# Attention scores in three fp32r passes, conv tails copied by GpSimd, an earlier first feed-forward, two loads moved and a new table of held steps in a hybrid decoder layer on one core

## The chip, the cores and the metric

One Trainium2 chip, one of its cores. The time of a run is device microseconds from the start to the end of the program on that core. Three runs of the kernel before took 3500.38, 3508.79 and 3495.04 us (median 3500.38). A change of 0.5% is 17.5 us.

## The reference, cut to what matters

One decoder layer is computed for a prompt of 2048 tokens and, beside it, for eight single sample tokens with caches. D = 1024, eight heads of 128: four of a gated DeltaNet group (a short convolution over time, then a delta-rule state) and four of a sparse attention group (two key-value heads; a lightning indexer chooses 256 keys for each query).

```python
qkv, z, beta_in, a_in, aq, ak, av, iq, ik, iw = jnp.split(h @ w_in, cuts, axis=-1)
conv = sum(w_conv[i] * xcat[:, i:i + t] for i in range(CONV_W))      # CONV_W = 4
...
s = jnp.einsum('bqgrd,bqkgd->bqgrk', qg, ks).astype(jnp.float32) * d ** -0.5
s = jnp.where(valid[:, :, None, None, :], s, -jnp.inf)
p = jax.nn.softmax(s, axis=-1).astype(vs.dtype)
...
x = x + ga1 * mixed
gate, up = jnp.split(h2 @ w_ffn_in, 2, axis=-1)
x = x + ga2 * ((jax.nn.silu(gate) * up) @ w_ffn_out)
```

The attention scores `s` are the product that the change computes in another way. For the prompt the kernel computes them for all keys up to the query and adds a bias of 0 or -1e30 that the indexer's selection gives.

## The kernel before, in words

**Tiles and stages.** The prompt is worked in four groups g of 512 tokens (`GT`). The stages are: modulation vectors; for each group the projections of the normed input by `w_in` (`project`), with the convolution, the delta rule in chunks of 128 tokens and the indexer's keys beside them; then for each group the output projection and the feed-forward (`ffn`), with the attention of 16 query blocks of 128 (`index`, `attend`) and the sample tokens' work beside them. Blocks 0 to 3 are attended early, during the projections (`first_attn`); blocks 4 to 15 in the second phase.

**Products.** Large products are done as three fp32r passes (`mm3`): both operands are split in a part that fp32r holds and the rest, and high by high, high by low and low by high are added in PSUM. In the profile these are L201, L202 and L203. A product whose operands are plain fp32 (the scores, L1799) is one matmul in the program, and two records of TensorE in the trace. A weight tile is loaded (`wr`, L183), cast by ScalarE to its high part (L184), and the rest taken by VectorE (L185); three pairs are kept (`WI`). The last feed-forward group uses a longer ring for pairs: `wi` and, in turns, tiles of the tags `kT` and `V`, which attention no longer needs, three of each (`KR`).

**Order.** `weave` runs several streams: `feeds` (projections, then feed-forwards), `chain` (delta rule, early attention), `toks` (rotary, transposes and stores of projected rows, from a queue), later `samples`, `indices` and `attends`. Each is a generator that yields a planned cost and a wait; the planner picks the next step that is able. The matmuls are then bound to stand on TensorE in exactly the order in which the steps came (`o`), so that a matmul whose data is late holds everything behind it. On the other engines and on SP, which issues nearly all DMAs, a scheduler orders the instructions. A table `DELAY` names, for a stream and a step's number, how many planned microseconds that stream is held after that step, so that other streams' steps go first.

**What the steps below touch.** `conv` reads a projected block from PSUM (`pd`, tag `d`, four banks): three ScalarE copies, of the last three columns of the group before (L975), of the block (L976) and of its own last three columns, from PSUM, to `hist` (L977). `tok` transposes the rotated queries and keys and stores them to `qT_d` and `kT_d` (L1030, L1048). `attend` loads them back (L1788, L1795), computes a score (L1799), and VectorE adds the bias and takes the maximum (L1800). `modulation` loads at the start, in SP's order, half of two parts of `w_ada` (`hh`, then `hl`) and the four row tiles of group 0 (`xt`, L336). `projects` ends with a wait for the queue of `toks` to be empty, and `ffn(0)` comes after it.

Of the kernel before, what the change touches and what calls it, by code (L numbers as in the profile page):

```python
# [20 lines left out]
try:  # L21
# [4 lines left out]
F32 = mybir.dt.float32  # L26
# [8 lines left out]
T = 2048  # L35
# [21 lines left out]
KR = 3  # L57
RB = 2
WR, WI = 2, 3
S2, S4, LATE = 8, 1044, 8000  # L60
# [6 lines left out]
    "attends": {18: 5.36, 27: 5.03, 43: 0.99},  # L67
    "chain": {6: 0.3, 7: 0.13, 16: 1.19, 44: 0.99, 45: 2.33, 48: 1.66, 57: 0.53, 62: 1.14, 110: 0.7, 112: 0.9, 124: 2.17, 162: 0.55, 163:
        0.36, 190: 0.44, 200: 0.23, 213: 0.85, 215: 3.15, 246: 0.89, 248: 2.32, 257: 3.29, 297: 0.55, 298: 0.36, 313: 0.29, 326: 1.4, 342:
        0.5, 354: 0.25, 442: 0.55, 443: 0.56, 455: 0.51, 460: 2.84, 461: 0.68, 483: 0.18, 492: 0.45, 508: 0.31, 515: 1.71, 517: 0.92, 536:  # L70
        0.21},
    "feeds": {1: 2.29, 14: 1.6, 27: 0.45, 101: 1.94, 182: 1.01, 451: 0.69, 457: 1.65, 588: 0.89, 714: 5.33, 902: 1.81, 903: 0.53, 1084:
        12.87, 1085: 0.65, 1197: 0.88, 1259: 1.05, 1290: 5.26, 1354: 0.8, 1355: 1.08, 1386: 1.28, 1389: 1.47, 1450: 2.45, 1451: 1.77, 1482:
        6.57},
    "indices": {2: 7.17},
    "samples": {2: 1.37, 4: 1.91, 8: 3.28, 13: 3.31, 17: 2.24, 29: 0.3, 40: 1.93},
    "toks": {1: 1.91, 5: 6.16, 79: 3.96, 106: 0.46, 134: 1.8, 136: 4.86, 184: 0.56, 193: 3.29, 229: 3.52, 231: 1.66, 239: 2.29, 241: 1.22,
        246: 1.66},
# [51 lines left out]
class K:  # L130
# [106 lines left out]
    def build(self):  # L237
        tc, nc = self.tc, self.nc
        with ExitStack() as es:
# [3 lines left out]
            self.qT_d = self.dr.tile([NB, 128, H * 128], F32, name="qT_d")  # L243
            self.iqT_d = self.dr.tile([NB, 128, 8 * 128], F32, name="iqT_d")
            self.kT_d = self.dr.tile([2, 128, T], F32, name="kT_d")
# [71 lines left out]
    def modulation(self):  # L317
# [17 lines left out]
        for t in range(4):  # L335
            nc.sync.dma_start(self.x0[:, t, :], A["x_prompt"][0, t * 128:(t + 1) * 128, :])  # L336
        self.load_ada(hl, 1, 0, 0, KB)
# [341 lines left out]
    def projects(self):  # L679
        nxt = None  # L680
        for g in range(self.ng):
# [59 lines left out]
    def project(self, g, rows):  # L741
# [10 lines left out]

        if samp:
# [4 lines left out]
        hidden(0)  # L758
        yield TP, 0.5
        hidden(1)  # L760
        yield TP, 2
# [4 lines left out]
        for c in range(3):  # L766
# [3 lines left out]
            for k in range(KB):  # L770
# [200 lines left out]
    def conv(self, g, m, pd):  # L971
# [3 lines left out]
        nc.scalar.copy(raw[:, 0:3], self.hist[:, m, :])  # L975
        nc.scalar.copy(raw[:, 3:515], pd)  # L976
        nc.scalar.copy(self.hist[:, m, :], pd[:, 509:512])  # L977
# [31 lines left out]
    def tok(self, what, blk, a, rows):  # L1009
# [8 lines left out]
        if what == "aq":  # L1018
# [9 lines left out]
            q = self.m("qo")[:, :512]  # L1028
            nc.scalar.copy(q, pt)
            nc.sync.dma_start(self.qT_d[blk], q)  # L1030
            yield TP, 0
        elif what == "kv":
# [13 lines left out]
            q = self.m("qo")[:, :512]  # L1046
            nc.scalar.copy(q[:, :256], pt[:, :256])
            nc.sync.dma_start(self.kT_d[:, :, tk].rearrange("h p n -> p h n"), q[:, :256].rearrange("p (h n) -> p h n", h=2))  # L1048
# [34 lines left out]


# [217 lines left out]
    def out_T(self, n, o):  # L1302
# [9 lines left out]
        raw = self.m("ol")[:, :512]  # L1312
# [22 lines left out]
    def sample_gdn(self):  # L1335
# [19 lines left out]
        for c in range(3):  # L1355
# [3 lines left out]
            yield 0, 4  # L1359
# [352 lines left out]
    def buffers(self):  # L1712
# [3 lines left out]
        return dict(pool=p, kT=one("kT", 512, KR), V=one("V", 512, KR), ikT=self.ikT, qT=one("qT", 512), iqT=one("iqT", 1024), sc=one("sc", T + 18, 2),  # L1716
# [3 lines left out]
    def first_attn(self, i0):  # L1720
# [8 lines left out]
        B = dict(pool=p, kT=one("E"), V=one("AT"), ikT=ikT, qT=one("qe"), iqT=one("sq", 1024), sc=lambda: p.tile([128, 528], F32, name="ct", tag="ct", bufs=4),  # L1729
# [53 lines left out]
    def attend(self, i, B, bias):  # L1783
# [3 lines left out]
        qT = B["qT"]().rearrange("p (h n) -> p h n", h=H)  # L1787
# [438 lines left out]
```

## Time and profile before

| | |
|---|---|
| the profiled execution | 3502.24 us |
| its span, first to last instruction | 3499.8 us |
| mean granted TensorE clock | 0.973 |
| TensorE busy | 3300.3 us, 94% of the span |
| TensorE weight loads, VectorE, ScalarE, GpSimd busy | 75%, 59%, 42%, 18% |
| moved by DMA | 549.7 MB, mean 157 GB/s |

Busy time of TensorE is the union of its records. A record lasts until the result has drained, while the next has begun, so a group's mean of 400 ns for a 512-column fp32r pass is no price: the price is the distance of starts. The granted clock of a stretch is 1.00 or, in parts, one half; a stretch's mean says how much of it was at half rate. Waits are those of the engine that is named first; "SPq" is the queue from which DMAs are issued. Line numbers are those of the kernel before, unless it is said that they are of the changed one.

### The profile page before, as it was taken

Reading aid. Unit: us, or ns where it says so; the run is one execution under the profiler, and the core shown is the slowest. Engines: PE = TensorE matmul, PEld = TensorE weight load, DVE = VectorE, ACT = ScalarE, POOL = GpSimd, SP = SyncE. Lnnn points to the kernel's source line nnn. Section 1 sums busy time; section 2 is a strip of 40 time slices with the busy share of each in tenths; the row PEclk is TensorE's granted clock in tenths of the full one; section 3 lists DMA queues with packets and bytes.
Section 4 is the critical chain, followed back from the end, with each engine's and each line's share of the span. In section 5 each row is a group of like instructions: output and inputs, shape, how many; then the busy total and the mean of one; then the engine's idle time right before and its main releaser. Section 6 shows DMA issues by size and latency. Waiting matters only on the chain.

```text
span 3499.8 us, 61968 instructions
## 1 busy us (share of the span) xinstructions
PE 3300.3 (94%) x22852; PEld 2623.9 (75%) x22852; DVE 2076.9 (59%) x4488; ACT 1470.0 (42%) x2875; POOL 640.8 (18%) x633
## 2 busy tenths in 40 slices
PE   7899998999998899999998999999899999999997
PEld 5677777777766777777776777787777777789996
DVE  4656545645744656666676656567766763554434
ACT  4333322423433333455546555454645553342323
POOL 1001000100000113221220122212112221324335
PEclk8999999999998999999999999999999999999999
DMA  8865764675786254455464345335423233622221
GB/s 287 272 204 167 247 210 147 220 244 171 230 282 208 92 163 120 138 168 166 125 212 139 102 144 171 106 105 197 143 88 113 91 111 94 202 82 88 88 91 56
DMA packets 421019, 549.70 MB, mean 157 GB/s; under 512 B 50020, under 2 KB 287817, under 8 KB 420698
## 3 DMA queue, kind: packets, MB, share of 16 engines
q1 hardware_dynamic: 420690, 545.62, 48.9%
q8 instruction: 182, 2.98, 0.4%
q14 instruction: 131, 1.07, 0.1%
q10 hardware_dynamic: 16, 0.03, 0.0%
HBM read 441.78 MB, written 122.70 MB: 161 GB/s over the span
## 4 chain that ended last, share of the span: by engine, by line
PE 71%; DMA 9%; DVE 9%; issue 5%; ACT 4%; SPq 1%; POOL 1%; ACTq 0%; DVEq 0%; POOLq 0%
PE d L201 16%; PE d L203 15%; PE d L202 15%; PE s L1754 3%; PE g L1816 3%; PE s L1799 3%; DMA wr<-in_w_ffn_in_dram 2%; DMA wi<-kept 1%; DVE wi L185 1%; PE g L1828 1%; PE s L202 1%; PE s L201 1%; PE s L203 1%; ACT bias L1623 1%; ACT wi L184 1%
## 5 line engine op out<-in xcount | busy, mean ns | idle before, releaser
L201 PE MATMUL d<-hh,wi 128*128 128x512 f32 (+1 forms) x1616 | 669.8, 414 | 20.2 <-DVE th L2153 7.6
L185 DVE TENSOR_TENSOR wi<-wr,wi 128x512 fp32r<-128x512 f32 x525 | 391.9, 747 | 396.9 <-ACT wi L184 392.4
L202 PE MATMUL d<-hl,wi 128*128 128x512 f32 (+1 forms) x1616 | 620.7, 384 | 4.7 <-DVE hl L506 4.4
L203 PE MATMUL d<-hh,wi 128*128 128x512 f32 (+1 forms) x1616 | 620.8, 384 | 0.0
L184 ACT CAST wi<-wr 128x512 fp32r<-128x512 f32 x525 | 324.6, 619 | 680.9 <-PE d L203 427.1
L201 PEld LDWEIGHTS d<-hh,wi 128*128 128x128 f32 x1616 | 308.3, 191 | 94.0 <-issue 11.7
L202 PEld LDWEIGHTS d<-hl,wi 128*128 128x128 f32 x1616 | 308.8, 191 | 68.4 <-issue 10.1
L203 PEld LDWEIGHTS d<-hh,wi 128*128 128x128 f32 x1616 | 307.6, 190 | 62.1 <-DVE wi L185 0.8
L201 PE MATMUL d<-wi,hh 128*128 128x512 f32 x736 | 317.6, 432 | 17.5 <-DMA wi<-kept 7.7
L202 PE MATMUL d<-wi,hh 128*128 128x512 f32 x736 | 291.9, 397 | 1.0 <-DVE wi L185 1.0
L203 PE MATMUL d<-wi,hl 128*128 128x512 f32 x736 | 292.4, 397 | 0.0
L201 PE MATMUL d<-wi,ah 128*128 128x512 f32 x616 | 267.9, 435 | 10.7 <-ACT ah L2161 5.0
L203 PE MATMUL d<-wi,al 128*128 128x512 f32 x616 | 246.9, 401 | 2.4 <-POOL al L2162 2.4
L202 PE MATMUL d<-wi,ah 128*128 128x512 f32 x616 | 245.9, 399 | 0.0
L2162 POOL TENSOR_TENSOR al<-ca,ah 128x512 fp32r<-128x512 f32 (+1 forms) x88 | 107.6, 1228 | 732.1 <-ACT ah L2161 698.3
L1763 DVE SCALAR_TENSOR_TENSOR sc<-rl,iw,sc 128x512 f32<-128x512 f32 (+3 forms) x224 | 173.3, 774 | 73.4 <-ACT rl L1756 67.8
L1891 POOL TENSOR_TENSOR xt<-xt,tm 128x512 f32<-128x512 f32 x96 | 136.9, 1441 | 426.3 <-DVE tm L1890 341.0
L1756 ACT ACTIVATE rl<-s 128x512 f32<-128x512 f32 (+3 forms) x288 | 151.5, 543 | 135.2 <-PE s L1754 126.6
L201 PEld LDWEIGHTS d<-wi,hh 128*128 128x128 f32 x736 | 140.3, 191 | 61.1 <-DMA wi<-kept 11.3
L1623 ACT ACTIVATE bias<-sc,sv 128x640 bf16<-128x640 f32 (+11 forms) x120 | 169.9, 1416 | 26.9 <-DVE sv L1625 15.1
L1754 PE MATMUL s<-ik,iqT 128*128 128x512 f32 (+3 forms) x576 | 171.2, 391 | 3.9 <-DVE st L1800 2.3
L203 PEld LDWEIGHTS d<-wi,hl 128*128 128x128 f32 x736 | 140.4, 191 | 32.2 <-issue 0.3
(587 smaller groups left out, 6323.8 us busy)
## 6 DMA issues: line engine op xcount, KB each, us to landing
wi<-kept SPq DMA_DIRECT2D x168, 512.0 KB
wr<-in_w_ffn_in_dram SPq DMA_DIRECT2D x584, 128.0 KB
wr<-in_w_ffn_out_dram SPq DMA_DIRECT2D x148, 256.0 KB
kept<-wi SPq DMA_DIRECT2D x56, 512.0 KB
row<-in_w_ada_dram SPq DMA_DIRECT2D x32, 512.0 KB
wr<-in_w_in_dram SPq DMA_DIRECT2D x56, 256.0 KB
xt<-in_x_prompt_dram SPq DMA_DIRECT2D x7, 2048.0 KB
kT<-kT_d SPq DMA_DIRECT2D x54, 256.0 KB
```

What stands on the lines that cost most here:

```text
L184: nc.scalar.copy(hi, wr)
L185: nc.vector.tensor_tensor(lo, wr, hi.bitcast(F32), op=OP.subtract)
L201: self.o(nc.tensor.matmul(out, wh, xh, start=start, stop=False, **kw))
L202: self.o(nc.tensor.matmul(out, wh, xl, start=False, stop=False, **kw))
L203: self.o(nc.tensor.matmul(out, wl, xh, start=False, stop=stop, **kw))
L1623: nc.scalar.activation(c, s, AF.Sign, bias=t, accum_out=cnt)
L1754: self.o(nc.tensor.matmul(ps[:, :w], iq[:, h, :].bitcast(F32R), B["ikT"][c * 2 + a][:, :w].bitcast(F32R), start=a == 0, stop=a == 1))
L1756: nc.scalar.activation(r[:, :w], ps[:, :w], AF.Relu)
L1763: nc.vector.scalar_tensor_tensor(s, r[:, :w], iw, s, op0=OP.mult, op1=OP.add)
L1799: self.o(nc.tensor.matmul(ps[:, :w], qT[:, h, :], kT[:, :w], start=True, stop=True))
L1891: (nc.vector if soon else nc.gpsimd).tensor_tensor(xt, xt, tm, op=OP.add)
L2162: nc.gpsimd.tensor_tensor(al[b][:, cs], a, ah[b][:, cs].bitcast(F32), op=OP.subtract)
```

## The change

- **Scores.** `parts` splits the transposed queries and keys in two fp32r parts (ScalarE casts, VectorE subtracts, both from PSUM); both are stored and loaded, so `qT_d`, `kT_d` and their loads double. The score is `mm3` in place of one fp32 matmul. Key tiles hold two parts each, and there are two of them (`RK`) in place of three; the last feed-forward's ring has two double tiles there in place of three pairs. To make room, the samples' tile ring goes from eight to six (`S2`).
- **Conv tails.** The two three-column copies go to GpSimd, and the second reads the SBUF copy instead of PSUM. `out_T` writes its raw tile over its input.
- **First feed-forward.** `projects` no longer waits for the queue; for the last group the modulation steps start earlier (`"mark"` in the conv loop); the gates' column has a tile of its own.
- **Moves.** At the start the second `w_ada` load goes ahead of the fourth row tile; the sample rows are prepared after the first two `hidden` tiles. The samples' first step is held 9 planned us instead of 4.
- **Table.** `DELAY` keeps its entries and gains or lengthens 55, by 69.7 planned us in sum. Steps of `feeds` are counted anew where steps were added, so old entries stand at up to some steps' distance from their old places.

```diff
-S2, S4, LATE = 8, 1044, 8000
+RK = 2
+S2, S4, LATE = 6, 1044, 8000
 DELAY = {
-    "attends": {18: 5.36, 27: 5.03, 43: 0.99},
+    "attends": {18: 5.36, 27: 5.03, 41: 2.04, 43: 0.99, 109: 1.17, 119: 0.16, 120: 0.98, 137: 0.48, 280: 0.28},
...
-    "samples": {2: 1.37, 4: 1.91, 8: 3.28, 13: 3.31, 17: 2.24, 29: 0.3, 40: 1.93},
+    "samples": {2: 1.37, 4: 1.91, 8: 7.09, 13: 3.31, 17: 2.24, 21: 5.15, 29: 0.3, 40: 1.93, 134: 0.53, 154: 1.89},
...
         for t in range(4):
+            if t == 3:
+                self.load_ada(hl, 1, 0, 0, KB)
             nc.sync.dma_start(self.x0[:, t, :], A["x_prompt"][0, t * 128:(t + 1) * 128, :])
-        self.load_ada(hl, 1, 0, 0, KB)
...
-                col = self.m("gate")
+                col = self.p1.tile([128, 8], F32, name="gcol", tag="gcol", bufs=1)
...
-        yield lambda: not self.queue
         self.ready.add("end")
...
                 if c == 0:
                     hidden(k + 2)
                     yield TP * (k + 2 < KB), 0
+                elif k % 2 and g == self.ng - 1:
+                    yield "mark"
...
-        nc.scalar.copy(raw[:, 0:3], self.hist[:, m, :])
+        nc.gpsimd.tensor_copy(raw[:, 0:3], self.hist[:, m, :])
         nc.scalar.copy(raw[:, 3:515], pd)
-        nc.scalar.copy(self.hist[:, m, :], pd[:, 509:512])
+        nc.gpsimd.tensor_copy(self.hist[:, m, :], raw[:, 512:515])
...
-            nc.scalar.copy(q, pt)
-            nc.sync.dma_start(self.qT_d[blk], q)
+            for e, q in enumerate(self.parts(pt, 512)):
+                nc.sync.dma_start(self.qT_d[blk, :, e], q)
...
+    def parts(self, pt, w):
+
+        nc = self.nc
+        hi, lo = [self.m("qo", F32R)[:, :w] for _ in range(2)]
+        nc.scalar.copy(hi, pt[:, :w])
+        nc.vector.tensor_tensor(lo, pt[:, :w], hi.bitcast(F32), op=OP.subtract)
+        return hi.bitcast(F32), lo.bitcast(F32)
...
-            yield 0, 4
+            yield 0, 4 if c else 9
...
-                nc.sync.dma_start(kT[:, :w], self.kT_d[kv, :, c * 512:c * 512 + w])
+                for e in range(2):
+                    nc.sync.dma_start(kT[e][:, :w].bitcast(F32), self.kT_d[kv, :, e, c * 512:c * 512 + w])
...
-                    self.o(nc.tensor.matmul(ps[:, :w], qT[:, h, :], kT[:, :w], start=True, stop=True))
+                    self.mm3(ps[:, :w], *[x[:, h * 128:(h + 1) * 128] for x in qT], *[x[:, :w] for x in kT], True, True)
...
-                    yield F4 * w / 512, 0, dict(dve=0.2 + 0.6 * w / 512, use="s", need="s")
+                    yield 3 * MM * w / 512, 0, dict(dve=0.2 + 0.6 * w / 512, use="s", need="s")
...
-            return [q.tile([128, 512], F32R, name=tag, tag=tag, bufs=KR) for tag in ("kT", "V")]
+            w = q.tile([128, 2, 512], F32R, name="kT", tag="kT", bufs=RK)
+            return w[:, 0], w[:, 1]
```

How the change moves instructions is shown at three places; names are those of tiles, and line numbers those of the kernel in question. Lines 201 to 203 of before are lines 203 to 205 of the changed kernel, and other lines move by 2 to 16.

**TensorE, end of the last projections.** Before, after the last projection's matmuls (`s<-cf,iqs`: transposes of `toks`; `g<-ct`, `g<-Dm,E`: the delta rule's chunks):

```order
L450 MATMUL s<-cf,m_11923 128x32 x4
L1183 MATMUL g<-cf,ct 128x128 x8
L1234 MATMUL g<-ct 128x256 x4
L1078 MATMUL s<-cf,iqs 128x128 x4
L1234 MATMUL g<-ct 128x256 x4
L1078 MATMUL s<-cf,iqs 128x128 x4
L1112 MATMUL g<-Dm,E 32x32 x32
```

The changed kernel, same place:

```order
L1245 MATMUL g<-ct 128x256 x4
L203 MATMUL d<-wi,hh 128x512
L204 MATMUL d<-wi,hh 128x512
L205 MATMUL d<-wi,hl 128x512
L1245 MATMUL g<-ct 128x256 x4
L1081 MATMUL s<-cf,iqs 128x128 x4
```

The first feed-forward's passes now stand between the steps of `chain` and `toks`, which stood alone.

**TensorE, a score of block 4 to 7.** Before, and then in the changed kernel:

```order
L1754 MATMUL s<-ik_14241,iqT 128x256
L1754 MATMUL s<-ik_14242,iqT 128x256
L1799 MATMUL s<-kT,qT 128x512
L201 MATMUL d<-wi,ah 128x512
L202 MATMUL d<-wi,ah 128x512
```

```order
L205 MATMUL d<-hh,wi 128x512
L203 MATMUL s<-kT,qT 128x512
L204 MATMUL s<-kT,qT 128x512
L205 MATMUL s<-kT,qT 128x512
L1419 MATMUL g<-s_17057,s_17966 128x1 x4
```

One score is three instructions; what stands beside it differs, since all streams' places have moved.

**SP, the first loads.** Before, and then in the changed kernel:

```order
L333 DMA gzc<-in_g_gdn_norm_dram 1x128
L336 DMA xt<-in_x_prompt_dram 128x1024 x4
L359 DMA hl<-in_w_ada_dram 128x4x512 x2
L339 DMA row<-in_x_sample_dram 8x1024
L183 DMA wr<-in_w_in_dram 128x512 x2
```

```order
L335 DMA gzc<-in_g_gdn_norm_dram 1x128
L340 DMA xt<-in_x_prompt_dram 128x1024 x3
L362 DMA hl<-in_w_ada_dram 128x4x512 x2
L340 DMA xt<-in_x_prompt_dram 128x1024
L342 DMA row<-in_x_sample_dram 8x1024
```

The second `w_ada` load stands one row tile earlier.

More of the change, by code (lines that the diff above doesn't have):

```diff
@@ L66 @@
 DELAY = {
[L67 to L78 removed]
+    "attends": {18: 5.36, 27: 5.03, 41: 2.04, 43: 0.99, 109: 1.17, 119: 0.16, 120: 0.98, 137: 0.48, 280: 0.28},
+    "chain": {5: 0.79, 6: 0.3, 7: 0.13, 16: 1.19, 19: 0.75, 44: 0.99, 45: 2.33, 48: 1.66, 56: 0.3, 57: 0.53, 61: 0.23, 62: 1.14, 85: 0.36,
[3 rows of a table added]
+    "feeds": {1: 2.29, 14: 1.6, 27: 0.45, 101: 1.94, 102: 1.07, 142: 2.08, 182: 1.01, 451: 0.69, 457: 1.65, 588: 0.89, 636: 1.12, 711: 0.69,
[3 rows of a table added]
+    "indices": {2: 7.17, 14: 5.43, 16: 1.62, 78: 0.28, 223: 2.29, 249: 0.54},
+    "samples": {2: 1.37, 4: 1.91, 8: 7.09, 13: 3.31, 17: 2.24, 21: 5.15, 29: 0.3, 40: 1.93, 134: 0.53, 154: 1.89},
+    "toks": {1: 1.91, 5: 6.16, 43: 0.47, 67: 0.56, 77: 0.18, 79: 3.96, 106: 1.56, 134: 1.8, 136: 4.86, 139: 0.82, 184: 0.56, 187: 0.56, 193:
+        3.29, 196: 0.45, 229: 3.52, 231: 1.66, 239: 2.29, 241: 1.22, 246: 1.66},
 }
@@ L751, in hidden @@
                 self.hidden_T(k, xt, hh, hl, self.A1, B1, "s", 2)
+        hidden(0)
+        yield TP, 0.5
+        hidden(1)
+        yield TP, 0.5
         if samp:
@@ L757, in project @@
             held = []
[L758 to L761, printed above, removed]
+        yield 0, 1.5
         def wtile(k, c0):
@@ L1045, in tok @@
                 return
-            q = self.m("qo")[:, :512]
-            nc.scalar.copy(q[:, :256], pt[:, :256])
-            nc.sync.dma_start(self.kT_d[:, :, tk].rearrange("h p n -> p h n"), q[:, :256].rearrange("p (h n) -> p h n", h=2))
+            for e, q in enumerate(self.parts(pt, 256)):
+                nc.sync.dma_start(self.kT_d[:, :, e, tk].rearrange("h p n -> p h n"), q.rearrange("p (h n) -> p h n", h=2))
             nc.sync.dma_start(self.V_d[tk], a[:, 256:512])
@@ L1311, in out_T @@
             self.o(nc.tensor.transpose(pt[:, hs(h)], o[:, hs(h)], self.id))
-        raw = self.m("ol")[:, :512]
+        raw = o
         lo = raw.bitcast(F32R)
@@ L1715, in buffers @@
         one = lambda tag, w, bufs=1, dt=F32: lambda: p.tile([128, w], dt, name=tag, tag=tag, bufs=bufs)
-        return dict(pool=p, kT=one("kT", 512, KR), V=one("V", 512, KR), ikT=self.ikT, qT=one("qT", 512), iqT=one("iqT", 1024), sc=one("sc", T + 18, 2),
+        two = lambda tag, bufs: lambda: (lambda x: [x[:, 0], x[:, 1]])(p.tile([128, 2, 512], F32R, name=tag, tag=tag, bufs=bufs))
+        return dict(pool=p, kT=two("kT", RK), V=one("V", 512, KR), ikT=self.ikT, qT=two("qT", 1), iqT=one("iqT", 1024), sc=one("sc", T + 18, 2),
                     bias=one("bias", T, 2, BF), big=one("big", T, 2), rl=one("rl", 512, 2),
@@ L1728, in first_attn @@
                 nc.sync.dma_start(ikT[a], self.ikT_d[a, :, :GT])
-        B = dict(pool=p, kT=one("E"), V=one("AT"), ikT=ikT, qT=one("qe"), iqT=one("sq", 1024), sc=lambda: p.tile([128, 528], F32, name="ct", tag="ct", bufs=4),
+        two = lambda *tags: lambda: [p.tile([128, 512], F32R, name=tag, tag=tag, bufs=2) for tag in tags]
+        B = dict(pool=p, kT=two("E", "NT"), V=one("AT"), ikT=ikT, qT=two("qe", "kd"), iqT=one("sq", 1024), sc=lambda: p.tile([128, 528], F32, name="ct", tag="ct", bufs=4),
                  bias=one("dec", 512, BF), big=one("Dm"), rl=one("decb"), PT=one("Y"), oT=one("v"))
@@ L1794, in attend @@
                 kT = B["kT"]()
-                nc.sync.dma_start(kT[:, :w], self.kT_d[kv, :, c * 512:c * 512 + w])
+                for e in range(2):
+                    nc.sync.dma_start(kT[e][:, :w].bitcast(F32), self.kT_d[kv, :, e, c * 512:c * 512 + w])
                 for r in range(2):
```

9 lines of the change are left out of this document (4 added, 5 removed), and 6 rows, old and new, of the table DELAY.

## The prediction, as recorded before the run

> **What bounds the kernel now.** I read the page's busy times first, then its rows of granted clock and of the chain that ended last.
>
> ```profile
> PE 3300.3 (94%) x22852; PEld 2623.9 (75%) x22852; DVE 2076.9 (59%) x4488; ACT 1470.0 (42%) x2875; POOL 640.8 (18%) x633
> PEclk8999999999998999999999999999999999999999
> PE 71%; DMA 9%; DVE 9%; issue 5%; ACT 4%; SPq 1%; POOL 1%; ACTq 0%; DVEq 0%; POOLq 0%
> ```
>
> TensorE is busy for 3300.3 of 3499.8 us. So there are two ways to be faster: less TensorE work, or less of the other 199.5 us together with what is lost to a lower clock. The clock loss is read from the table of stretches (from:to and length, busy us and count of TensorE, its weight loads, VectorE, ScalarE and GpSimd, granted clock, DMA share, GB/s), which I asked for the whole and then for the places where TensorE waits longest:
>
> ```profile
> 30.00:3477.00 3447.00, 3284.55 (x22775) 2616.20 (x22776) 2057.37 (x4452) 1451.21 (x2832) 621.17 (x602) 0.98 0.49 156
> 1082.60:1123.15 40.55, 24.55 (x354) 17.65 (x353) 22.53 (x70) 12.49 (x29) 2.09 (x2) 0.76 0.72 232
> 1291.00:1295.30 4.30, 0.43 (x2) 0.00 (x0) 0.69 (x1) 0.62 (x1) 0.73 (x2) 0.97 0.89 310
> 1295.30:1302.00 6.70, 6.42 (x21) 5.04 (x22) 2.18 (x4) 1.73 (x3) 0.00 (x0) 0.51 0.91 289
> 2486.00:2500.00 14.00, 6.11 (x24) 3.97 (x23) 8.88 (x22) 12.76 (x20) 1.87 (x2) 0.63 0.56 170
> ```
>
> At a mean clock of 0.98, about 0.02 x 3285 = 66 us go to half rate. The third and fourth rows show where from: 4.30 us with almost no matmul at clock 0.97, then 6.70 us of solid work at 0.51. A wait of some 4 us thus costs about 3 us more behind it (6.42 x 0.49). The Trainium skill, "TensorE: Matmul & The Clock Gate", Part 1, says that an idle window of about 3.4 us halves the clock and that about as long a busy one restores it; the trace agrees with the first and shows up to twice the second.
>
> **The scores.** What is removed is 160 fp32 matmuls, 112 of them 512 wide and 16 each of 384, 256 and 128; 160 times three fp32r passes are added. Price from the order of starts on TensorE, and the groups' rows for the count:
>
> ```profile
> 2867.02 1.88 PE L1799 MATMUL s<-kT,qT 128*128 128x512 f32 x4
> 2868.33 0.79 PE L201 MATMUL d<-wi,ah 128*128 128x512 f32 x1
> 2868.97 0.39 PE L202 MATMUL d<-wi,ah 128*128 128x512 f32 x1
> 2869.19 0.39 PE L203 MATMUL d<-wi,al 128*128 128x512 f32 x1
> 2869.43 0.39 PE L201 MATMUL d<-wi,ah 128*128 128x512 f32 x1
> ...
> L1799 PE MATMUL s<-kT,qT 128*128 128x512 f32 x216 | 106.4, 594 | 3.0 <-DVE st L1800 2.7 <-ACT rl L1756 0.3
> L1799 PE MATMUL s<-kT,qT 128*128 128x384 f32 x24 | 9.4, 486 | 0.0
> ```
>
> The 216 records are 108 scores; early block 3 has four more under other tile names. One fp32r pass is 2869.43 - 2869.19 = 0.23 (rounded). Two scores and the L201 after them take 2868.97 - 2867.02 = 1.95 us, so a score takes (1.95 - 0.23) / 2 = 0.86, against 3 x 0.23 = 0.69. 112 x 0.17 = 19 us less. For the 48 narrower ones, -4 us if the saving scales with width (16 x 0.17 x 1.5), +12 if no pass were shorter than a full one (16 x 0.78); I take -1, which is what passes give that halve but get no shorter. Scores lie on the bound engine: **-20**.
>
> The split adds one VectorE subtract per transposed tile (16 of 512 columns, 16 of 256) and twice the stores and loads of q and k. No row has such a subtract from PSUM; at most it is L185's 747 ns on the page, 12 us on VectorE for the wide ones, which is busy 59%. That is hidden unless `toks` is what a matmul waits for; the doubled issues on SP are costed below.
>
> **Conv tails.** The banks of the last projection pass are given back by ScalarE's L977. ScalarE (as its records show) does the four block copies first:
>
> ```profile
> 107.58 0.59 ACT L976 COPY raw<-d 128x512 f32<-128x512 f32 x1
> ...
> 110.81 0.27 ACT L977 COPY hist<-d 128x3 f32<-128x3 f32 x2
> 111.07 0.79 PE L201 MATMUL d<-hh,wi 128*128 128x512 f32 x1 [4.01 <-ACT hist L977]
> ...
> 140.46 0.59 ACT L976 COPY raw<-d 128x512 f32<-128x512 f32 x1
> 143.42 0.50 PE L201 MATMUL d<-wi,hh 128*128 128x512 f32 x1 [3.69 <-ACT hist L977]
> ...
> 111.07:117.80 6.73, 6.73 (x24) 5.30 (x25) 6.67 (x18) 4.45 (x12) 0.00 (x0) 0.78 0.47 156
> 143.40:150.20 6.80, 6.78 (x25) 4.97 (x26) 6.77 (x13) 2.04 (x6) 0.00 (x0) 0.75 0.58 191
> ...
> L1523 POOL COPY s<-qTs 128x4 f32<-128x4 f32 x8 | 1.0, 192 | 0.1
> ```
>
> In the changed kernel nothing but L976 reads the bank. The first bank is then free at 107.58 + 0.59 = 108.17 instead of 111.07 (2.9 us), at the other place at 140.46 + 0.59 = 141.05 instead of 143.42 (2.4). With the clock behind them, 6.73 x 0.22 + 6.80 x 0.25 = 3.2, that is up to 8.5; the waits in whole with the clock are 10.9. I take **-8**, bounds 0 to -11. The 96 small copies at 192 ns are 18 us on GpSimd, busy 18%. The Trainium skill, "GPSIMD Engine Reference", section 1 Specifications, says that GpSimd's SBUF interfaces are shared with VectorE and contended by VectorE instructions with two SBUF inputs, which the convolution's steps are; by that the copies could cost up to the same 18 us of VectorE. No row shows it, and VectorE has room: 0 in the sum.
>
> **The drain.** Between 1082.6 and 1123.15 (row above) the last `chain` and `toks` steps stand alone on TensorE. Work is 24.55 x 0.76 = 18.7 us at full rate, so 21.9 of 40.55 us are lost, for instance here:
>
> ```profile
> 1101.48 3.78 PE L1234 MATMUL g<-ct 128*128 128x256 f32 x8 [2.56 <-DVE v L1221]
> ```
>
> Now the first feed-forward's passes stand between them. What is late next is the first pair of its inputs and weights, one wait like the 4.3 us at the start (below). So **-18**, bounds 0 (the passes only wait there in place of the others) and -22.
>
> **Held steps and moves.** At the start TensorE waits twice for `hl`, the load that moves ahead of the fourth row tile:
>
> ```profile
> 14.00:30.00 16.00, 8.80 (x41) 4.88 (x41) 8.04 (x20) 7.38 (x19) 1.97 (x3) 0.53 1.04 382
> ...
> 18.04 1.94 PE L408 MATMUL g<-hl,cT 128*32 128x512 f32 x8 [4.33 <-DMA hl<-in_w_ada_dram]
> 29.83 0.79 PE L201 MATMUL d<-hh,wi 128*128 128x512 f32 x1 [0.70 <-ACT hh L505]
> ```
>
> The load comes one row tile (0.52 MB, 1.4 us at that stretch's 382 GB/s) earlier, but that tile is then later and TensorE needs it before 29.83: **-2**, bounds 0 and -4.3. The samples' first wait (the third and fourth stretch above) and two behind it:
>
> ```profile
> PE g L1362 <- DMA s<-in_state_conv_dram: 4.2, 1, 4.2
> PE g L1385 <- DVE s L1389: 3.3, 1, 3.3
> PE g L1417 <- DVE s L1412: 3.2, 2, 1.9
> ```
>
> 10.7 us and 3.1 of clock. Three entries of the table (8 and 21 of `samples`, and the 9 in place of 4) put other matmuls there: **-8** of 14, bounds 0 and -14. In the third feed-forward's norm (stretch 2486 to 2500) work is 6.11 x 0.63 = 3.9, so 10.1 us are lost; a new entry holds the feed-forward there, attention goes first: **-6**, bounds 0 and -10. The other entries stand among small waits such as these, some at displaced steps:
>
> ```profile
> PE d L201 <- DMA wi<-kept: 11.5, 9, 2.5
> PE d L201 <- DVE th L2153: 8.6, 9, 3.3
> ```
>
> I take 0. Of the 199.5 us without TensorE some 47 are in the terms above and 37 in the first 30 and the last 23 us; a third of the other 115 is -38, and +23 is a third of the 69.7 us held, with nothing else able to go.
>
> **Keys just in time.** With two key tiles a load can start only when the chunk before the last has been consumed, and it is now two issues:
>
> ```profile
> 2655.49 0.93 SPq L183 DMA_DIRECT2D wr<-in_w_ffn_out_dram  x2
> 2658.23 0.62 ACT L184 CAST wi<-wr 128x512 fp32r<-128x512 f32 x1 [1.08 <-DMA wr<-in_w_ffn_out_dram]
> ...
> 2870.12 1.88 PE L1799 MATMUL s<-kT,qT 128*128 128x512 f32 x4
> 2872.54 1.88 PE L1799 MATMUL s<-kT,qT 128*128 128x512 f32 x4
> ...
> SPq L183 <- DVE wi L185: 765.3, 325, 8.2
> SPq L1795 <- PE s L1799: 60.5, 36, 5.1
> ```
>
> Two loads of this size take 2.74 us from the first issue to use, 3.2 with a second issue's time. Chunks follow one another here by 3.10 and 2.42 us, so a third or fourth chunk (24 loads: one chunk more in blocks 8 to 11 and two in 12 to 15, for two key-value heads) can be late by up to about a microsecond, and more if SP stands in a weight's wait, up to 8.2. Elsewhere attention steps are spread between feed-forward steps. I take **+4**, bounds 0 and 24 x 3.2 = +77; the doubled q and k traffic and the shorter ring at the end (DMA share 0.49 overall): **+2**, bounds 0 and +10.
>
> **Sum.** -20 - 18 - 2 - 8 - 8 - 6 + 6 = -56. The profiled execution took 3502.24 us, 1.9 above the median of the three runs: 3502 - 56 = **3446 us**.
>
> **Rivals.** A change of 0.5% is 17.5 us, about what a measurement of this kernel can tell; faster is below 3482.9, slower above 3517.9.
>
> *Only the scores come through.* TensorE's order is fixed, and a wait removed is often given to the next late operand: while VectorE is 59% busy, chains of its small steps end somewhere. For it: most of the 199.5 us is in waits as small as the two just shown. Against it: the drain and the conv waits have other, ready matmuls to put there. 3502 - 20 = 3482, 3470 to 3490.
>
> *Keys just in time (slower).* One mechanism, at L1795: each of 24 loads is late in whole, because SP stands before a weight load that waits for VectorE (765.3 us in 325 waits, 2.4 each) when the key tile comes free. 3446 + 77 - 4 = 3519. Beyond (56 + 4) / 24 = 2.5 us of mean lateness it is slower than before. Against it: most attention steps have feed-forward passes between them, and VectorE's waits of SP overlap with what the planner puts there.
>
> *The clock.* If the held steps leave no wait long enough to halve the clock, the 66 us, less what the terms above count (24.55 x 0.24 + 3.2 + 3.1 + 6.11 x 0.37 = 14.5), come back: 3446 - 51 = 3395. Against it: the row of the clock stands at 8 or 9 in nearly every slice, so the waits are everywhere and 55 entries don't reach them all. By the skill's rule (its Part 1, above) every wait must fall below a window for this.
>
> *The weights queue behind stores at the drain.* The change does there what it says, and gains nothing: SP takes its instructions in order, and now the first feed-forward's weights stand behind stores of the last `toks`:
>
> ```profile
> SPq L1081 <- ACT iqs L1073: 69.9, 18, 11.4
> ```
>
> With one such wait of 11.4 and several of the mean 3.9, the 18 us of the drain are gone: 3446 + 18 = 3464.
>
> **How the numbers follow.** The sum holds with 0.52 (its own range 3415 to 3475, where the small terms' bounds lie), only the scores 0.24, the queue at the drain 0.08, slower by keys 0.09, the clock 0.07. Faster: 0.52 + 0.08 + 0.07, and half of the second case's 0.24, whose middle lies on the threshold: 0.79. Within 0.5%: the other half, 0.12. Slower: 0.09. The range leaves out most of the clock's case below and the keys' case above, and holds the scores' case whole: 3405 to 3495.
>
> **What would show it.** The score's three passes 0.69 us apart, and no idle time before them behind a key load; no wait of TensorE for L977's successor; the stretch of the last projections without 20 us lost, with ffn passes at a clock above 0.9; no 4 us wait for `in_state_conv`; less than 10 us lost in the third norm. It is wrong if SP's waits at the key loads come out of TensorE's time, if the lost time reappears as waits for the first feed-forward's norm, or if the sum of TensorE's busy time falls by less than 20 us.

## The result, and the profile after

The changed kernel took 3469.73 us (median of five runs, 3463.18 to 3475.96) against 3500.79 for the kernel before (five runs). The ratio is 0.9912, 95% interval 0.9891 to 0.9933: 31 us faster, 23 to 38. The forecast was 56 us faster, 3446. Executions in a second, slower state are left out of all medians and ratios here (one of them, with the table of before, took 4592.98 us at a mean clock of 0.652).

The profiled execution of the changed kernel took 3463.18 us, the lowest of its five, that of before 3502.24. Between the two profiles there are thus 39 us, of which 8 are only the places of these two executions among their kernels' runs. The page's line of busy times, of the changed kernel:

```profile
PE 3270.4 (94%) x23012; PEld 2637.8 (76%) x23012; DVE 2079.9 (60%) x4520; ACT 1460.1 (42%) x2779; POOL 672.4 (19%) x729
PEclk9999999999999999999999999999999999999998
```

TensorE is busy 29.9 us less (3300.3 before), and the rest of the span falls from 199.5 to 3461.4 - 3270.4 = 191.0, that is by 8.5 us, about what the choice of executions makes. So the part of the forecast that is TensorE's own came: three passes in place of an fp32 matmul, and less time at half rate. What did not come is the waits: some 20 us that the sum took from them are back in other places. First a score in the changed kernel, in order of starts on TensorE (L203 to L205 are the three passes):

```profile
2841.42 0.39 PE L203 MATMUL s<-kT,qT 128*128 128x512 f32 x1
2841.65 0.40 PE L204 MATMUL s<-kT,qT 128*128 128x512 f32 x1
2841.89 0.39 PE L205 MATMUL s<-kT,qT 128*128 128x512 f32 x1
...
2842.81 0.40 PE L203 MATMUL d<-wi,ah 128*128 128x512 f32 x1
```

Two scores take 2842.81 - 2841.42 = 1.39 us, 0.69 each, as the sum had it. Now waits of TensorE in the changed kernel, the ones that matter here (us in total, times, longest):

```profile
PE d L203 <- DMA wi<-kept: 18.3, 11, 4.0
PE s L505 <- DVE xt L498: 17.5, 7, 7.2
PE d L203 <- DVE th L2169: 12.9, 9, 3.8
...
PE d L203 <- DMA hh<-oTh_d: 4.9, 1, 4.9
...
PE g L1452 <- ACT PT L1846: 4.1, 1, 4.1
PE g L1194 <- DMA ct<-cT_d: 4.1, 1, 4.1
...
PE d L203 <- ACT raw L981: 2.4, 2, 1.3
```

The waits for `hist` (7.7), `hl` (5.5) and `in_state_conv` (4.2) are gone. In their place: the projections' weights that are kept in DRAM (`wi<-kept`), 18.3 instead of 11.5; `th`, 12.9 instead of 8.6; two new waits of 4 us, for `ct` in the projections (a load right behind the spot where the tails' wait went) and for `PT` in the samples' work. The tails leave a wait of 1.3 us for the block copy (L981), as worked out. The drain's stretch shows what the prediction expected behind it, the first pair of `hh` and `hl`:

```profile
1082.85 0.77 PE L203 MATMUL d<-wi,hh 128*128 128x512 f32 x1 [4.87 <-DMA hh<-oTh_d]
1084.80 0.80 PE L205 MATMUL d<-wi,hl 128*128 128x512 f32 x1 [0.76 <-DMA hl<-oTl_d]
...
1082.60:1123.15 40.55, 39.43 (x478) 31.19 (x478) 24.87 (x63) 15.45 (x35) 6.44 (x6) 0.90 0.55 185
```

(The last row is the table of stretches over the same 40.55 us as before: 39.43 us busy at clock 0.90, where it was 24.55 at 0.76. So 40.55 - 39.43 x 0.90 = 5.1 us are lost in it. The wait of 4.87 us lies nearly all ahead of the stretch; with it some 10 us are lost, against 21.9 before, though not all work in the two stretches is the same.) The third feed-forward's norm is the place that went the wrong way:

```profile
2466.81 0.69 PE L505 MATMUL s<-cf,xt 128*128 128x128 f32 x2 [7.23 <-DVE xt L498]
2471.88 1.54 PE L505 MATMUL s<-cf,xt 128*128 128x128 f32 x6 [4.38 <-DVE xt L498]
2475.17 0.79 PE L203 MATMUL d<-hh,wi 128*128 128x512 f32 x1 [1.75 <-ACT hh L508]
...
2454.00:2480.00 26.00, 12.64 (x48) 9.19 (x47) 25.03 (x40) 9.96 (x20) 3.58 (x4) 0.67 0.40 117
```

13.4 us of waits; in the whole stretch 26.00 - 12.64 x 0.67 = 17.5 us are lost, where the prediction counted 10.1 before and wanted 6 of them back. The kernel before has 7.3 us of waits there, the first of them just ahead of the norm:

```profile
2489.68 2.06 PE L1816 MATMUL g<-PT,V 128*128 128x256 f32 x4 [2.21 <-ACT PT L1831]
2493.38 0.47 PE L502 MATMUL s<-cf,xt 128*128 128x128 f32 x1 [1.64 <-DVE xt L495]
2495.34 0.48 PE L502 MATMUL s<-cf,xt 128*128 128x128 f32 x1 [1.49 <-ACT xt L493]
2497.80 0.48 PE L502 MATMUL s<-cf,xt 128*128 128x128 f32 x1 [1.98 <-DVE sv L1624]
```

In the changed kernel VectorE is busy 25.03 of 26 us: the norm's scaling (L498) stands behind the selection of the next attention block, in steps of 2 us on 1792 columns, as its own records show:

```profile
2464.61 1.21 DVE L1906 TENSOR_TENSOR xt<-xt,ca 128x512 f32<-128x512 f32 x1
...
2466.02 0.74 DVE L498 TENSOR_SCALAR xt<-xt,rnz 128x1024 f32<-128x1024 f32 x1
2466.68 2.01 DVE L1649 MAX8 sv<-sc 128x8 f32<-128x1792 f32 x1
...
2469.01 2.02 DVE L1653 MATCH_REPLACE8 sc<-sv,sc 128x1808 f32<-128x1808 f32 x1
...
2471.08 0.74 DVE L498 TENSOR_SCALAR xt<-xt,rnz 128x1024 f32<-128x1024 f32 x1
```

### The profile page after: what moved, and what is told of

It reads as the page before. It is cut to its first block, busy times and chain, and to the rows that moved or that the text cites. A ratio compares the mean times of both kernels' runs of the same rounds, so it can differ in the third digit from the quotient of the medians.

```text
span 3461.4 us, 62636 instructions
## 1 busy us (share of the span) xinstructions
PE 3270.4 (94%) x23012; PEld 2637.8 (76%) x23012; DVE 2079.9 (60%) x4520; ACT 1460.1 (42%) x2779; POOL 672.4 (19%) x729
## 4 chain that ended last, share of the span: by engine, by line
PE 69%; DMA 10%; DVE 9%; issue 6%; ACT 4%; SPq 2%; POOL 1%; ACTq 0%; DVEq 0%; POOLq 0%
PE d L203 16%; PE d L205 15%; PE d L204 15%; PE s L1767 3%; PE g L1831 2%; PE s L203 2%; PE s L204 2%; PE s L205 2%; DMA wi<-kept 2%; DVE wi L187 1%; DMA wr<-in_w_ffn_in_dram 1%; PE g L1843 1%; ACT bias L1634 1%; DMA wr<-in_w_out_dram 1%; DMA wr<-in_w_in_dram 1%
## 5 line engine op out<-in xcount | busy, mean ns | idle before, releaser
L203 PE MATMUL d<-hh,wi 128*128 128x512 f32 (+1 forms) x1616 | 649.9, 402 | 16.4 <-DMA wi<-kept 3.8
L205 PE MATMUL d<-hh,wi 128*128 128x512 f32 (+1 forms) x1616 | 618.9, 383 | 0.5 <-DVE wi L187 0.5
L203 PEld LDWEIGHTS d<-hh,wi 128*128 128x128 f32 x1616 | 306.9, 190 | 83.9 <-issue 7.7
L205 PEld LDWEIGHTS d<-hh,wi 128*128 128x128 f32 x1616 | 306.0, 189 | 62.5 <-DVE wi L187 1.7
L203 PE MATMUL d<-wi,hh 128*128 128x512 f32 x736 | 315.7, 429 | 26.1 <-DMA wi<-kept 14.5
L205 PE MATMUL d<-wi,hl 128*128 128x512 f32 x736 | 293.9, 399 | 1.1 <-DMA hl<-oTl_d 0.8
L203 PE MATMUL d<-wi,ah 128*128 128x512 f32 x616 | 252.3, 410 | 14.4 <-DVE th L2169 9.8
L205 PE MATMUL d<-wi,al 128*128 128x512 f32 x616 | 243.5, 395 | 2.7 <-POOL al L2178 2.7
L204 PE MATMUL d<-wi,ah 128*128 128x512 f32 x616 | 243.9, 396 | 0.0
L203 PEld LDWEIGHTS d<-wi,hh 128*128 128x128 f32 x736 | 141.8, 193 | 65.7 <-DMA wi<-kept 18.4
L205 PEld LDWEIGHTS d<-wi,hl 128*128 128x128 f32 x736 | 142.0, 193 | 33.8 <-DMA hl<-oTl_d 1.5
```

Source lines behind the costliest of these rows:

```text
L203: self.o(nc.tensor.matmul(out, wh, xh, start=start, stop=False, **kw))
L204: self.o(nc.tensor.matmul(out, wh, xl, start=False, stop=False, **kw))
L205: self.o(nc.tensor.matmul(out, wl, xh, start=False, stop=stop, **kw))
```

## The experiments

Each was timed in five rounds beside the kernel before, which is why ratios are given; 0.01 is 35 us. The theory to test was the prediction's sum; the rivals were that the scores cost more than their price (keys just in time, rings, splits), and that the order of the steps, which the change moves, costs or gives what the sum had put down to its parts.

**The scores alone.** All edits of the scores on the kernel before: `parts`, the doubled `qT_d` and `kT_d`, the two double key tiles, six sample tiles, and

```diff
-self.o(nc.tensor.matmul(ps[:, :w], qT[:, h, :], kT[:, :w], start=True, stop=True))
+self.mm3(ps[:, :w], *[x[:, h * 128:(h + 1) * 128] for x in qT], *[x[:, :w] for x in kT], True, True)
...
-yield F4 * w / 512, 0, ...
+yield 3 * MM * w / 512, 0, ...
```

> The kernel before with the scores' part of the change alone: both parts of q and k stored and loaded, three passes, two double key tiles, six sample tiles, old table, nothing moved. If the score's price is what matters (112 x 0.17 us and the narrow ones): 3480, between 3472 and 3488. If the just-in-time keys or the displaced interleaving eat it: 3492 to 3510.

3534.67 us, ratio 1.0114 (1.0097 to 1.0131): 40 us slower, where -14 was forecast with its keys and rings. This is the step of the sum that failed; the next question is which part of the edit does it: the passes, the splits with their doubled loads, the rings or the planned cost.

**The table of before in the changed kernel.** The diff is `DELAY` alone.

> The changed kernel with the table of held steps of before. If the new entries bring what the prediction counted for the samples' waits and the third norm (8 + 6 us) or more: 3484 to 3500. If the new entries take as much as they give, or sit at displaced steps: 3462 to 3477.

3506.83 us, ratio 1.0033 (1.0016 to 1.0050). All else in the change, on top of the scores, is thus worth 1.0114 - 1.0033 = 0.0081, 28 us, which is what was forecast for drain, tails and load (18 + 8 + 2). The new entries are worth 1.0033 - 0.9912 = 0.0121, 42 us, where 14 were forecast. Both are differences of ratios that are known to 6 or 7 us each, and the old entries stand at displaced steps here, so part of the 42 may be their displacement.

**The wait for the queue put back.**

```diff
+        yield lambda: not self.queue
         self.ready.add("end")
+DELAY["feeds"] = {k + (k >= 1091): v for k, v in DELAY["feeds"].items()}
```

> The changed kernel with the wait for the empty queue put back at the end of the projections (the table's entries behind it are counted on by one step, so they stay at their places). If the drain's term is real: 18 us slower, 3480 to 3490. If the drain's waits only moved to the steps around it: 3464 to 3476.

3502.62 us, ratio 1.0011 (1.0000 to 1.0022): 35 us slower than the changed kernel, about twice the term. The drain's own stalls are back, here in the order of starts on TensorE:

```profile
1081.27 0.75 PE L1083 MATMUL s<-cf,iqs 128*128 128x128 f32 x4 [2.20 <-DVE iqs L1079]
1085.94 3.78 PE L1247 MATMUL g<-ct 128*128 128x256 f32 x8 [3.92 <-DVE v L1234]
...
1095.09 0.66 PE L1083 MATMUL s<-cf,iqs 128*128 128x128 f32 x4 [1.74 <-DVE iqs L1079]
```

Not all of it is the drain. The two profiled executions differ by 32 us (spans of 3493.6 and 3461.4), and 22 of these stand when the second feed-forward's norm starts on TensorE (1843.1 us here, 1820.9 in the changed kernel), after 14781 and 14733 of its matmul records. The other 10 come later, where the steps stand in another order than the one that the table's entries were set for.

**The tails back on ScalarE.**

```diff
-        nc.gpsimd.tensor_copy(raw[:, 0:3], self.hist[:, m, :])
+        nc.scalar.copy(raw[:, 0:3], self.hist[:, m, :])
         nc.scalar.copy(raw[:, 3:515], pd)
-        nc.gpsimd.tensor_copy(self.hist[:, m, :], raw[:, 512:515])
+        nc.scalar.copy(self.hist[:, m, :], pd[:, 509:512])
```

> The changed kernel with the two three-column copies of the convolution back on ScalarE, the second from PSUM. If the tails' term is real: 8 us slower, 3475 to 3481. If the new order of the steps hides the tail anyway: 3466 to 3473.

3480.50 us, ratio 0.9947 (0.9933 to 0.9962): 12 us slower, the two intervals just touching, with TensorE's order unchanged by the trace. The waits are back at the very places:

```profile
107.52 0.79 PE L203 MATMUL d<-hh,wi 128*128 128x512 f32 x1 [4.00 <-ACT hist L982]
141.16 0.79 PE L203 MATMUL d<-wi,hh 128*128 128x512 f32 x1 [3.69 <-ACT hist L982]
```

**Without the hold at the third norm.** The entry `2363: 5.78` of `feeds` is taken out.

> The changed kernel without the one entry that holds the feed-forward 5.78 planned us ahead of the third norm (feeds, 2363). If the third norm is worse than before because of it: 6 us or more faster, 3456 to 3464. If the hold helps and the norm's wait comes from VectorE's selection steps that now stand ahead of it: 3468 to 3480.

3474.78 us, ratio 0.9933 (0.9918 to 0.9948), not to be told from the changed kernel. Its third norm waits 7.21, 4.38 and 1.76 us, as with the hold. So this entry neither causes that wait nor cures it.

**The rings alone.** On the kernel before: two key tiles in place of three, also in the last feed-forward's ring, and six sample tiles in place of eight.

```diff
-S2, S4, LATE = 8, 1044, 8000
+RK = 2
+S2, S4, LATE = 6, 1044, 8000
...
-kT=one("kT", 512, KR)
+kT=one("kT", 512, RK)
...
-... name=tag, tag=tag, bufs=KR) for tag in ("kT", "V")]
+... name=tag, tag=tag, bufs=RK if tag == "kT" else KR) for tag in ("kT", "V")]
```

> The kernel before with only the rings made smaller: two key tiles in place of three (in attention and in the last feed-forward's ring), six sample tiles in place of eight; scores as before. The scores alone with their rings took 3534.7, about 37 more than before. If the just-in-time keys and the smaller rings cost it: 3525 to 3555. If the rings cost nothing here and the cost is in the order or the splits: 3495 to 3505.

3502.99 us, ratio 1.0009 (0.9998 to 1.0021): at most 7 us, about 3. Smaller rings with single loads are not the 40; what the doubled loads add to them is not in this run.

**Three passes, and nothing else of the scores.** Single loads, old rings, no low parts (`q` and `k` are rounded to fp32r when they are stored, and their tiles are fp32r); planned cost as in the change.

```diff
-self.o(nc.tensor.matmul(ps[:, :w], qT[:, h, :], kT[:, :w], start=True, stop=True))
+self.mm3(ps[:, :w], qT[:, h, :], qT[:, h, :], kT[:, :w], kT[:, :w], True, True)
...
-yield F4 * w / 512, 0, ...
+yield 3 * MM * w / 512, 0, ...
```

> The kernel before with three fp32r passes for each score, but of q and k rounded to fp32r, with no low parts: the low parts' products are left out (the same tile is used for both), so there are no subtracts, no doubled stores and loads, and the rings are as before. What is left is the price of three passes and the planned cost that moves the order. If TensorE's price comes through: 3476 to 3486. If the table of before no longer fits once the order moves: 3500 to 3540, and the cost of the scores is in the order, not in rings or loads.

3522.84 us, ratio 1.0066 (1.0051 to 1.0081): 23 us slower with cheaper matmuls and no added load. That leaves the planned cost, the one line of the edit that computes nothing. Two more runs complete the square.

**The same passes with the old planned cost, and the new planned cost without the passes.** The first is the run above without the `yield` line, the second is the kernel before with the `yield` line alone.

> As the three unsplit passes before (low parts' products left out, the high tile used in their place), but with the planned cost of a score left at that of the fp32 matmul, so that the steps come in the order of the kernel before. If the 23 us that the three unsplit passes lost were the order's: the score's price comes through, 3474 to 3488. If the passes themselves cost it: 3515 to 3530, as there.

> The kernel before, scores as fp32 matmuls, with only the planned cost of a score set to that of three passes: nothing is computed in another way, the order of the steps moves. If the order costs it: 23 + 20, that is 3530 to 3555. If the order is no matter: 3493 to 3506.

| | planned 0.88 a score (order of before) | planned 0.69 (order moved) |
|---|---|---|
| fp32 matmul | 1 | 1.0114 (1.0099 to 1.0129), 3534.78 us |
| three passes | 0.9978 (0.9968 to 0.9987), 3486.15 us | 1.0066 (1.0051 to 1.0081), 3522.84 us |

The right column against the left: 40 us slower in the first row, 31 in the second, for a number that only the planner reads. The lower row against the upper: 8 us faster, and 17. So the passes do gain, and the order took it and more. That the planned cost acts through the order is borne out by the traces: TensorE's operations come in one and the same order in the kernel before, the rings alone and the passes with the old cost, and in one and the same other order in the new cost alone, the unsplit passes and the scores alone.

The square leaves a third part. The scores alone (1.0114) have the order and the passes of the unsplit ones (1.0066); what they have besides, splits, doubled stores and loads and smaller rings, costs 0.0048, some 17 us (known to 8), and so eats the 17 that the passes gain there: the scores alone are no faster than the new planned cost alone.

The page's busy times, first with the passes in the old order, then with the new planned cost alone:

```profile
PE 3275.2 (94%) x23012; PEld 2644.1 (76%) x23012; DVE 2080.1 (60%) x4488; ACT 1468.7 (42%) x2875; POOL 640.1 (18%) x633
...
PE 3309.7 (94%) x22852; PEld 2623.3 (74%) x22852; DVE 2069.1 (59%) x4488; ACT 1470.0 (42%) x2875; POOL 644.9 (18%) x633
```

The passes in the old order: TensorE is busy 25.1 us less (the score's price, some of it clock), and the rest of the span of 3483.2 is 208.0 instead of 199.5: 8.5 us given back in waits even where every step stands as before. The pair of executions thus differs by 16.6 us, while the ratios say 8 (5 to 11); the latter is used below. The planned cost alone: 9.4 us more busy, and of 3532.4 us 222.7 without TensorE, 23 more. The greatest single wait there is the third norm again, on TensorE, with the stretches of the wait and behind it:

```profile
2523.12 1.30 PE L502 MATMUL s<-cf,xt 128*128 128x128 f32 x3 [10.73 <-DVE xt L495]
...
2512.40:2523.10 10.70, 0.00 (x0) 0.00 (x0) 10.06 (x17) 4.30 (x10) 2.32 (x3) 0.63 0.59 196
2523.10:2532.00 8.90, 7.92 (x20) 5.31 (x21) 3.66 (x5) 2.75 (x4) 0.02 (x2) 0.50 0.00 0
```

No matmul in 10.7 us, then 8.9 us at half rate: 19.60 - 7.92 x 0.50 = 15.6 us are lost here, 5.5 more than before. That is the smaller part of the 33 us by which this execution is longer. 13 of them stand already when the second norm starts (1867.9 against 1854.9 us); they were not traced to single waits. How far attention is when the third norm comes can be counted: matmuls of weights by values (L1816, L1831 in the changed kernel) from the start to the first of the third norm's transposes, in the kernel before, the passes in the old order, the planned cost alone, and the changed kernel (columns: from:to length, busy and count of TensorE and of its weight loads, clock, DMA share, GB/s):

```profile
0.00:2493.30 2493.30, 90.55 (x342) 59.79 (x342) 0.97 0.56 179
```
```profile
0.00:2479.60 2479.60, 90.61 (x342) 60.16 (x342) 0.98 0.57 180
```
```profile
0.00:2523.10 2523.10, 98.06 (x364) 64.77 (x364) 0.97 0.56 178
```
```profile
0.00:2466.80 2466.80, 96.47 (x364) 63.63 (x364) 0.98 0.61 191
```

342 in the old order, 364 in the moved one. A score that is planned 0.19 us cheaper lets attention, and with it the selection of the next block, run ahead of the feed-forward in the plan. In the kernel before the 22 matmuls stand behind the norm's first eight transposes (from 2500.82 us on), so it is not they that shorten its waits. What differs at the waits is VectorE: before, the same selection of 1792 columns is still at its counts on ScalarE (L1623), with steps of 0.15 and 0.22 us on VectorE, and the first step of 2 us begins at 2504.80 us, behind the norm's scaling; in the moved order these steps stand ahead of it. The changed kernel has the same 364 and the same meeting of norm and selection, which its new entries don't mend. The run with the wait for the queue put back shows no wait of its third norm for the scaling, and is 35 us slower all the same: the norm is a place where the order's loss shows, not its whole price.

**One pass of the three.** In the changed kernel, with the order and the planned costs kept.

```diff
-self.mm3(ps[:, :w], *[x[:, h * 128:(h + 1) * 128] for x in qT], *[x[:, :w] for x in kT], True, True)
+self.o(nc.tensor.matmul(ps[:, :w], qT[0][:, h * 128:(h + 1) * 128], kT[0][:, :w], start=True, stop=True))
```

> The changed kernel, same order and planned costs, with one pass of the three (high by high) for each score: the other two, 112 x 0.46 us and some 13 us of narrow ones, are left out, and so is the low parts' contribution. If TensorE's time in attention counts in full: 64 us faster, 3400 to 3412. If other engines or loads are waited for as soon as TensorE has less to do: 3425 to 3465.

3425.27 us, ratio 0.9782 (0.9763 to 0.9800), 46 us faster than the changed kernel. TensorE is busy 3206.5 us by the page, 63.9 less. So of TensorE time that is taken away in attention, in a fixed order, about 70% comes through (46 of 64, known to some 10 us); the passes in the old order gave 8 (5 to 11) of the 20 that they were priced at, less than that.

Some 6 of the 46 are won at the third norm, and they show what it waits for. TensorE's order is that of the changed kernel, with the same 364 matmuls ahead of the norm. But VectorE gets to the norm's first scaling (L498) ahead of the selection's steps of 2 us, where it stands behind two of them in the changed kernel, and to the second behind one, where it stands behind four:

```profile
2430.42 0.75 DVE L498 TENSOR_SCALAR xt<-xt,rnz 128x1024 f32<-128x1024 f32 x1 [0.56 <-POOL rnz L477]
2431.96 2.08 DVE L1640 TENSOR_SCALAR_CACHE_REDUCE bias<-sc,sv 128x1792 bf16<-128x1792 f32 x1
2433.96 0.75 DVE L498 TENSOR_SCALAR xt<-xt,rnz 128x1024 f32<-128x1024 f32 x1
```

The waits of the first transposes and the first pass are 3.17, 1.31, 1.42, 1.09 and 0.74 us, 7.7 instead of 13.4. So it is the selection's long steps that lengthen this wait, and not the matmuls that are gone.

**The norm first.** In the changed kernel, in feed-forwards 0 to 2:

```diff
+        def first(yes):
+            return self.tc.high_priority(offset=EARLY) if yes else nullcontext()
...
-            self.scale_rows(xt, ms, True)
+            with first(True):
+                self.scale_rows(xt, ms, True)
```

and the same priority around the second half's residual add, its squares and the first two transposed tiles.

> The changed kernel; in feed-forwards 0 to 2 the second half's residual add, the squares, the row scaling and the first two transposed tiles of the norm are given priority on their engines, ahead of the selection's 2 us steps that stand before the third norm's scaling. If those steps are what the third norm waits for: some 10 us faster, 3454 to 3464, and less than 8 us lost in the third norm. If the delayed selection is then waited for: 3468 to 3480.

3466.05 us, ratio 0.9918 (0.9906 to 0.9930), no difference to be told. But the waits of the third norm are 7.21, 4.38 and 1.75 us, and the selection's steps still stand ahead of the scaling on VectorE: the priority did not change the order there, so the run doesn't test it. By the run with one pass, some 6 us are to be had there.

**The whole score part in the order of before.** All edits of the scores with the planned cost left at `F4`, the tails on GpSimd and the earlier load; old table.

> The kernel before with the scores' part in full (both parts, doubled loads, smaller rings), the tails on GpSimd and the earlier load, old table, and the planned cost of a score left at the fp32 matmul's, so that the order of before stays. If prices come through once the order stays: 3500 - 20 - 11 - 2, that is 3460 to 3476. If the splits and doubled loads cost something themselves: 3480 to 3495.

3505.37 us, ratio 1.0022 (1.0010 to 1.0033): not the 3460 to 3476 of the prices. TensorE's order is that of the kernel before and of the unsplit passes, by the trace. It is 15 us slower than the unsplit passes in the same order, though it has the tails besides. Matched start by start on TensorE, its profiled execution is 10 us ahead of theirs at 138 us (the tails and the earlier load), level at 1291, 8 behind at 2148, 18 behind at 2411 and 22 at the end. So the tails' gain is given back while the projections run; the splits and doubled stores stand there, but that they are the cause was not followed wait by wait. The greatest single step behind that is a key load:

```profile
PE s L203 <- DMA kT<-kT_d: 10.4, 3, 9.1
...
2392.01 0.33 SPq L1807 DMA_DIRECT2D kT<-kT_d  x1
...
2399.60 3.04 SPq L1807 DMA_DIRECT2D kT<-kT_d  x3
...
2410.08 0.79 PE L203 MATMUL s<-kT,qT 128*128 128x512 f32 x1 [9.11 <-DMA kT<-kT_d]
...
2396.00:2410.00 14.00, 4.96 (x22) 3.73 (x20) 5.40 (x10) 3.65 (x8) 3.30 (x2) 0.76 0.91 326
```

The first half of the key tile is issued at 2392.01, the second only at 2399.60: between them SP issues the third feed-forward's `hh` and `hl` loads and waits. The second half is used 10.5 us after its issue, with the DMA engines 0.91 busy in that stretch. The keys' rival exists, then, in one order of the steps, and both parts of its mechanism are in it, the doubled issue on SP and the load of the DMA engines; in the changed kernel's waits no key load appears.

## Why the prediction was right or wrong

The direction and the range held (3470 in 3405 to 3495), and faster was clear; the size was 31 of 56 us. That the sum came this near is luck: one step missed by 54 us, another by 28 the other way. The time alone would as well fit the rival "only the scores come through" (3470 to 3490), and the runs show the opposite of that rival. Along the three steps that the runs allow, in us against the kernel before:

| step | forecast | measured |
|---|---|---|
| the scores with splits, loads, rings, planned cost | -14 | +40 |
| with drain, tails, load and the other moves | -28 | -28 |
| with the new table | -14 | -42 |
| sum | -56 | -31 |

The second row agrees as a sum of its parts; by themselves, undone in the changed kernel, they come out greater (below).

**Scores.** The price was right: 0.69 against 0.86 us, start to start. The step that failed is "Scores lie on the bound engine: -20". It took TensorE's busy share of 94% for an exchange of one to one. In the kernel before's order 8 us came; and the change doesn't keep that order, because the planned cost goes down with the real one. This term, +40 by itself, was in no part of the sum. And the splits with their doubled traffic, which were put down as hidden, cost some 17 us with the rings in the moved order. The prediction's sentence that the planner's order makes "a wait removed ... given to the next late operand" was the nearest to it, but as a rival in which holds fail, with a price of zero on top of the scores.

**Keys just in time, rings.** +4 and +2 were forecast. The smaller rings alone cost about 3; with the doubled loads and the splits it is some 17, and how these share it is open. The rival's 77 us was far off: the greatest wait of that kind was one of 9 us, in another order.

**Conv tails.** -8 forecast, 12 when undone, which the intervals don't tell from 8; the mechanism, both places and the 1.3 us left are as worked out.

**The drain.** -18 forecast, 35 when undone, of which by the traces about 22 belong to the drain and what stands up to the second norm, and the rest to the order behind; the new wait of 4.87 us for the first pair is the 4.3 that was named. The rival of weights queued behind stores falls: TensorE waits for `hh` there, for no weight, and is then busy for 39.43 of 40.55 us.

**Held steps.** The samples' 4.2 us wait went, and 4.15 came behind `PT` further on. The third norm was taken at -6 because an entry holds the feed-forward there; its waits went from 7.3 to 13.4 us, and without the entry they are the same. The error was to read a hold as cover: a hold gives time to streams that have steps to give, and with the hold or without it 364 of attention's matmuls are done when the norm comes. The "other entries" stood at 0 with bounds -38 and +23. As all new entries bring 42 where 14 were counted, the other ones bring some 28 or more, but against the table of before in an order that it was not made for. That most of the new entries repair the order that the cheaper score upset is likely by this, but no run shows it. (By the diff there are 57 new or longer entries, not 55.)

**The clock.** Mean 0.979 against 0.973 in the two profiled executions; the kernel before has 0.972 to 0.981 in its runs beside the experiments, so part of the difference is the choice of executions. The rival of no halved stretch falls: the third norm's stretch still has a mean of 0.67.

## What to carry to other kernels

Where a planner sets the order of a bound engine from cost estimates, a cheaper instruction is two changes, its time and its number in the plan: time each by itself (new work with the old number, the new number with the old work) before the price is put into a sum. A busy share of 94% says that time on that engine is dear, not that every microsecond taken from it comes back; where the freed time lies beside a chain on another engine (here the norm and the selection on VectorE), it becomes a wait. And a hold pays only as long as another stream has work left for it, which can be counted in the trace. A split of operands that is "hidden" on engines with room has a price too: put it into the sum, or time the passes with and without it.

## What the runs showed of the hardware

The three-column copies take GpSimd nearly twice what was assumed from a copy of four columns (192 ns), because they wait for VectorE; and VectorE does not pay for them. Groups by shape in the changed kernel up to 1120 us for GpSimd and up to 1100 for VectorE, then the same VectorE step with the tails back on ScalarE:

```profile
L982 POOL COPY hist<-raw 128x3 f32<-128x3 f32 x48 | 16.8, 352 | 133.4 <-ACT raw L981 132.7
L980 POOL COPY raw<-hist 128x3 f32<-128x3 f32 x48 | 14.5, 337 | 23.3 <-DVE ca L987 17.5 <-DMA ikT_d<-ikT 3.1 <-PE s L453 2.6
L987 DVE SCALAR_TENSOR_TENSOR ca<-raw,cv,ca 128x512 f32<-128x512 f32 x144 | 102.6, 743 | 0.5
```
```profile
L987 DVE SCALAR_TENSOR_TENSOR ca<-raw,cv,ca 128x512 f32<-128x512 f32 x144 | 103.5, 747 | 0.6
```

31 us on GpSimd, with VectorE's steps at 743 ns beside them and at 747 without. The Trainium skill, "GPSIMD Engine Reference", section 1 Specifications, would let copies on GpSimd contend with just these two-input steps. The trace agrees, and the one that waits here is GpSimd, not VectorE, as the prediction had it for a possibility. The copies by themselves (count, shortest, median and longest ns), and a place where two of them meet three of VectorE's steps:

```profile
L982 POOL COPY hist<-raw x48: 187/286/772, 66.5 to 936.4; 128x3 f32<-128x3 f32 x48
L980 POOL COPY raw<-hist x48: 175/188/725, 48.2 to 920.7; 128x3 f32<-128x3 f32 x48
...
132.64 1.35 POOL L982 COPY hist<-raw 128x3 f32<-128x3 f32 x2 [0.30 <-ACT raw L981]
132.54 2.06 DVE L987 SCALAR_TENSOR_TENSOR ca<-raw,cv,ca 128x512 f32<-128x512 f32 x3
```

49 of the 96 copies take 175 to 191 ns, which is what was assumed. Each of the other 47 ends 30 to 60 ns behind the end of a VectorE step in which it stood, most of them of the convolution (L987, and L985 with one input in SBUF): the copy waits the step out, up to 772 ns in all.

That freed time on an engine busy 94% was worth between 40% (8 of the 20 us priced) and 70% (46 of 64) in a fixed order was also not expected; the two runs differ in the order that is fixed and in the amount, and which of these makes the difference was not tried.
